# Rotary embedding on one core: the first batch row loaded by one GpSimd cast transfer instead of two transfers on two queues

## The chip, the cores and the metric

One core of one Trainium2 chip. The metric is device time in microseconds (us), the median of several runs of the whole kernel, inputs and outputs in HBM.

## The reference

The kernel rotates pairs of neighbouring elements. `x` is 8 x 2048 x 16 x 64 in fp32 (batch, sequence, heads, head size), `cos` and `sin` are 2048 x 32:

```python
x_pairs = x.reshape(batch, seq_len, num_heads, head_dim // 2, 2)
x1 = x_pairs[..., 0]
x2 = x_pairs[..., 1]
out1 = x1 * cos - x2 * sin      # cos, sin: one value per position and pair
out2 = x1 * sin + x2 * cos
out = np.stack([out1, out2], axis=-1).reshape(batch, seq_len, num_heads, head_dim)
```

`x` and `out` are 67.1 MB each.

## The kernel before

The sequence is split over 128 partitions, 16 positions on each, so a batch row of `x` is a tile of 128 x 16384 elements: 8.39 MB in fp32 in HBM, half of that in bf16 in the core. The kernel works in bf16. A transfer issued by GpSimd (the helpers `load` and `store`) changes fp32 to bf16 on the way in and back on the way out.

`xt` holds five such rows (slots); `HOME` says which slot each of the eight batch rows uses, so rows 5, 6 and 7 go into the slots of rows 0, 1 and 2 once those are stored. `c_tab` and `s_tab` hold the cosines and signed sines in bf16, each value twice. `rotate(b)` does three VectorE instructions on a row: L89 writes `qt` = x * `s_tab`, L92 writes x = x * `c_tab` in place, L97 adds `qt` with the neighbours swapped to x. `qt` is one buffer of the pool `stage`.

The order is written out by hand (`manual_schedule`); each engine does its instructions in the order of the code.

- Head: the first row comes in two parts. Positions 0 to 3 of each partition (`HEAD` = 4, 2.10 MB of fp32) are loaded by SyncE without a cast (L101) into the buffer `head` (named `st` in the profile), which shares its room with `qt`, and ScalarE casts them into `xt` (L108). Positions 4 to 15 come by a GpSimd cast transfer (L102). Behind that on GpSimd's queue stand cos (L103), sin (L104), rows 1 and 2 in one transfer (`load(1, 2)`, L70), and rows 3 and 4 (`load(3, 2)`).
- VectorE builds the tables (L110 to L112), then does rotate(0) in two pieces (positions 0 to 3, then 4 to 15), then rows 1 to 7 in one piece each.
- Stores by GpSimd (L74): row 0 is issued behind the first instruction of rotate(2), through two one-element ScalarE copies (L120, L121) that hold it back; rows 1 and 2 after rotate(2); rows 3 and 4 after rotate(4); rows 5 and 6 after rotate(6). Row 5 is loaded once row 0 is stored, rows 6 and 7 once rows 1 and 2 are.
- End: ScalarE casts row 7 to fp32 in four parts (L138) into the room of slots 3 and 4, and SyncE stores it (L139).

Of the kernel before, what the change touches and what calls it, by code (L numbers as in the profile page):

```python
# [2 lines left out]

# [4 lines left out]


@with_exitstack  # L10
def kernel(
    ctx: ExitStack,
    tc: tile.TileContext,
    x: bass.AP,
    cos: bass.AP,
    sin: bass.AP,
    out: bass.AP,
):
    nc = tc.nc
    fp32 = mybir.dt.float32  # L20
    bf16 = mybir.dt.bfloat16
    mult = mybir.AluOpType.mult
    add = mybir.AluOpType.add

    B, S, H, D = x.shape
    P = 128
    K = S // P
    KP = 16
    D2 = D // 2
    HD = H * D  # L30
    NX = 5
    HEAD = 4
    PART = 4
    STAGE = 3


    HOME = [0, 1, 2, 3, 4, 0, 1, 2]

    x_t = x.rearrange("b (p k) h d -> b p k (h d)", p=P, k=K)
    out_t = out.rearrange("b (p k) h d -> b p k (h d)", p=P, k=K)  # L40
    x_r = x.rearrange("b (p k) h d -> p b (k h d)", p=P, k=K)
    out_r = out.rearrange("b (p k) h d -> p b (k h d)", p=P, k=K)
    cos_t = cos.rearrange("(p k) c -> p (k c)", p=P, k=K)
    sin_t = sin.rearrange("(p k) c -> p (k c)", p=P, k=K)

    consts = ctx.enter_context(tc.tile_pool(name="consts", bufs=1))
    stage = ctx.enter_context(tc.tile_pool(name="stage", bufs=1))

    xt = consts.tile([P, NX, K * HD], bf16)
    cos_sb = consts.tile([P, K * D2], fp32)  # L50
    sin_sb = consts.tile([P, K * D2], fp32)
    c_tab = consts.tile([P, K, D], bf16)
    s_tab = consts.tile([P, K, D], bf16)

    wide = (
        xt[:, STAGE : STAGE + 2]
        .rearrange("p a c -> p (a c)")
        .bitcast(fp32)
        .rearrange("p (k c) -> p k c", c=HD)
    )  # L60

    gate = consts.tile([1, 1], bf16)
    mark = consts.tile([1, 1], bf16)

    def home(b, k0=0, k1=K):
        return xt[:, HOME[b], k0 * HD : k1 * HD].rearrange("p (k c) -> p k c", c=HD)

    def load(b, n):
        h = HOME[b]
        nc.gpsimd.dma_start(out=xt[:, h : h + n], in_=x_r[:, b : b + n])  # L70

    def store(b, n):
        h = HOME[b]
        nc.gpsimd.dma_start(out=out_r[:, b : b + n], in_=xt[:, h : h + n])  # L74

    def rotate(b, k0=0, k1=K, between=None):
        nk = k1 - k0
        xp = home(b, k0, k1)
        qt = stage.tile([P, KP, HD], bf16, name="qt", tag="work")

        def rows(a):
            return a.rearrange("p k (h e) -> p k h e", h=H, e=D)

        def tab(a):
            return dataclasses.replace(
                a, offset=a.offset + k0 * D, ap=[a.ap[0], [D, nk], [0, H], [1, D]]
            )

        nc.vector.tensor_tensor(out=rows(qt[:, :nk]), in0=rows(xp), in1=tab(s_tab), op=mult)  # L89
        if between is not None:  # L90
            between(qt)
        nc.vector.tensor_tensor(out=rows(xp), in0=rows(xp), in1=tab(c_tab), op=mult)  # L92
        q_swap = dataclasses.replace(
            qt, offset=qt.offset + 1, ap=[qt.ap[0], [2, nk * HD // 2], [-1, 2]]
        )
        x3 = xp.rearrange("p k (a j) -> p (k a) j", j=2)
        nc.vector.tensor_tensor(out=x3, in0=x3, in1=q_swap, op=add)  # L97

    with tc.manual_schedule():
        head = stage.tile([P, HEAD, HD], fp32, name="st", tag="work")  # L100
        nc.sync.dma_start(out=head[:, :HEAD], in_=x_t[0, :, :HEAD])  # L101
        nc.gpsimd.dma_start(out=home(0, HEAD), in_=x_t[0, :, HEAD:])  # L102
        nc.gpsimd.dma_start(out=cos_sb, in_=cos_t)  # L103
        nc.gpsimd.dma_start(out=sin_sb, in_=sin_t)  # L104
        load(1, 2)
        load(3, 2)

        nc.scalar.copy(out=home(0, 0, HEAD), in_=head[:, :HEAD])  # L108
        s2 = s_tab.rearrange("p k (i j) -> p (k i) j", j=2)
        nc.vector.tensor_copy(out=s2[:, :, 0], in_=sin_sb)  # L110
        nc.vector.tensor_scalar_mul(s2[:, :, 1], sin_sb, -1.0)  # L111
        nc.vector.tensor_copy(  # L112
            out=c_tab.rearrange("p k (i j) -> p (k i) j", j=2),
            in_=cos_sb.to_broadcast([P, K * D2, 2]),
        )
        rotate(0, 0, HEAD)
        rotate(0, HEAD, K)

        def first_store(qt):
            nc.scalar.copy(out=gate, in_=qt[:1, KP - 1, HD - 1 :])  # L120
            nc.scalar.copy(out=xt[:1, HOME[0], :1], in_=xt[:1, HOME[0], :1])  # L121
            store(0, 1)

        rotate(1)
        rotate(2, between=first_store)
        nc.gpsimd.tensor_copy(out=mark, in_=xt[:1, 4, K * HD - 1 :])  # L126
        store(1, 2)
        load(5, 1)
        load(6, 2)
        rotate(3)  # L130
        rotate(4)
        store(3, 2)
        for b in range(5, B):
            rotate(b)
            if b == 6:
                store(5, 2)
        for k in range(0, K, PART):
            nc.scalar.copy(out=wide[:, k : k + PART], in_=home(B - 1, k, k + PART))  # L138
        nc.sync.dma_start(out=out_t[B - 1], in_=wide)  # L139


# [1 line left out]
_INS = ['x', 'cos', 'sin']  # L143
_OUTS = [((8, 2048, 16, 64), 'float32')]


# [23 lines left out]
```

## Time and profile before

| | |
|---|---|
| median of 3 runs | 316.28 us (316.09 to 316.48) |
| span of the profiled execution, first to last instruction | 314.3 us |
| the median stands above that span by | 1.98 us |
| busy in the span | VectorE 210.3 us, ScalarE 19.3 us, GpSimd 12.4 us |
| transfers, counted as written | GpSimd's queue (q0) 91.75 MB, SyncE's (q1) 10.49 MB |

The profile gives no separate time for its own execution; its span is set against the median of the runs. In the profile DVE is VectorE, ACT is ScalarE, POOL is GpSimd and SP is SyncE; a letter q behind an engine means its queue. The DMA share is the mean over the core's 16 DMA engines, in the rows by slices in tenths, in the rows by stretches as a fraction. A transfer's packets are counted where they start, so a very short stretch can show a share above 1. A wait is put down to what ended it.

### The profile page before, as it was taken

How to read it: one execution, taken by the hardware profiler on the slowest of the kernel's cores; microseconds unless marked ns; L12 is line 12 of the kernel's file. 1: busy time of each engine (PE TensorE's matmuls, PEld its weight loads, DVE VectorE, ACT ScalarE, POOL GpSimd, SP SyncE). 2: the span in 40 equal slices, each digit the busy share in tenths (PEclk: the TensorE clock that was granted, in tenths of full speed). 3: DMA queues.
4: the chain of work that ended last, by engine and by line, in shares of the span. 5: the costliest groups of instructions: out<-in, count | busy, mean ns of one | idle time of the engine just before them, and what ended most of it. 6: DMA issues, size and time to landing. Idle time of an engine off the chain costs nothing.

```text
span 314.3 us, 114 instructions
## 1 busy us (share of the span) xinstructions
DVE 210.3 (67%) x30; ACT 19.3 (6%) x8; POOL 12.4 (4%) x16
## 2 busy tenths in 40 slices
DVE  0009995099999999999992299903999999200000
ACT  1030000000000000000000000000000000790000
POOL 4000000000002400000000000000000000000000
DMA  7999999999999999999999999999999999999996
GB/s 253 264 284 200 200 200 267 200 200 204 263 200 267 409 525 400 400 425 509 400 200 225 242 200 200 234 234 334 400 509 425 400 400 525 409 400 400 525 409 267
DMA packets 2512, 102.24 MB, mean 325 GB/s; under 512 B 208, under 2 KB 208, under 8 KB 336
## 3 DMA queue, kind: packets, MB, share of 16 engines
q0 software_dynamic: 2224, 91.75, 92.1%
q1 hardware_dynamic: 288, 10.49, 8.0%
HBM read 67.63 MB, written 67.11 MB: 429 GB/s over the span
## 4 chain that ended last, share of the span: by engine, by line
DVE 67%; another core or an unknown queue 11%; ACT 3%; ACTq 1%; issue 0%; DVEq 0%
DVE xt L92 22%; DVE xt L97 22%; DVE qt L89 22%; ACT xt L138 3%; ACTq L165 1%; DVE c_tab L112 0%; DVEq L89 0%; DVEq L92 0%
## 5 line engine op out<-in xcount | busy, mean ns | idle before, releaser
L89 DVE TENSOR_TENSOR qt<-xt,s_tab 128x16384 bf16<-128x16384 bf16 (+2 forms) x9 | 69.7, 7743 | 34.5 <-DMA xt<-in_x_dram 34.3
L92 DVE TENSOR_TENSOR xt<-xt,c_tab 128x16384 bf16<-128x16384 bf16 (+2 forms) x9 | 69.7, 7743 | 0.4
L97 DVE TENSOR_TENSOR xt<-xt,qt 128x16384 bf16<-128x16384 bf16 (+2 forms) x9 | 69.7, 7743 | 0.3
L138 ACT CAST xt<-xt 128x4096 f32<-128x4096 bf16 x4 | 14.1, 3601 | 171.7 <-DVE xt L97 171.7
L110 DVE CAST s_tab<-sin_sb 128x512 bf16<-128x512 f32 x1 | 0.5, 454 | 23.8 <-DMA sin_sb<-in_sin_dram 23.8
L74 POOL DMA_DIRECT2D out_dram<-xt x4 | 2.7, 670 | 184.9 <-ACT xt L121 93.4
L126 POOL COPY mark<-xt 1x1 bf16<-1x1 bf16 x1 | 5.0, 5019 | 2.6 <-DMA xt<-in_x_dram 2.6
L120 ACT COPY gate<-qt 1x1 bf16<-1x1 bf16 x1 | 0.2, 192 | 78.6 <-DVE qt L89 78.6
L70 POOL DMA_DIRECT2D xt<-in_x_dram x4 | 2.7, 696 | 43.1 <-DMA out_dram<-xt 43.1
L108 ACT CAST xt<-st 128x4096 bf16<-128x4096 f32 x1 | 3.6, 3605 | 13.1 <-DMA st<-in_x_dram 13.1
L108 ACT ACT_TABLE_LOAD x1 | 1.3, 1283 | 0.7 <-PEq L154 0.7
L102 POOL DMA_DIRECT2D xt<-in_x_dram x1 | 0.7, 680 | 0.8 <-PEq L165 0.8
L112 DVE CAST c_tab<-cos_sb 128x1024 bf16<-128x1024 f32 x1 | 0.7, 685 | 0.0
L103 POOL DMA_DIRECT2D cos_sb<-in_cos_dram x1 | 0.6, 569 | 0.0
L104 POOL DMA_DIRECT2D sin_sb<-in_sin_dram x1 | 0.6, 562 | 0.0
L111 DVE TENSOR_SCALAR s_tab<-sin_sb 128x512 bf16<-128x512 f32 x1 | 0.4, 444 | 0.0
L121 ACT COPY xt<-xt 1x1 bf16<-1x1 bf16 x1 | 0.2, 188 | 0.0
L154 POOL MEMSET const-float32-0.0<- 128x1 f32 x1 | 0.1, 99 | 0.2 <-issue 0.2
L154 POOL MEMSET const-bfloat16-1.0<- 128x1 bf16 x1 | 0.1, 102 | 0.0
L154 POOL MEMSET const-float32-1.0<- 128x1 f32 x1 | 0.1, 99 | 0.0
L154 POOL MEMSET const-uint8-127<- 128x1 uint8 x1 | 0.1, 99 | 0.0
## 6 DMA issues: line engine op xcount, KB each, us to landing
xt<-in_x_dram POOLq DMA_DIRECT2D x3, 8192.0 KB, 59.3
xt<-in_x_dram POOLq DMA_DIRECT2D x1, 4096.0 KB, 57.6
xt<-in_x_dram POOLq DMA_DIRECT2D x1, 3072.0 KB, 21.1
st<-in_x_dram SPq DMA_DIRECT2D x1, 2048.0 KB, 14.4
cos_sb<-in_cos_dram POOLq DMA_DIRECT2D x1, 256.0 KB, 21.2
sin_sb<-in_sin_dram POOLq DMA_DIRECT2D x1, 256.0 KB, 21.3
out_dram<-xt POOLq DMA_DIRECT2D x4, 49.9
out_dram<-xt SPq DMA_DIRECT2D x1, 30.0
```

The costliest lines, as they stand in the source:

```text
L70: nc.gpsimd.dma_start(out=xt[:, h : h + n], in_=x_r[:, b : b + n])
L74: nc.gpsimd.dma_start(out=out_r[:, b : b + n], in_=xt[:, h : h + n])
L89: nc.vector.tensor_tensor(out=rows(qt[:, :nk]), in0=rows(xp), in1=tab(s_tab), op=mult)
L92: nc.vector.tensor_tensor(out=rows(xp), in0=rows(xp), in1=tab(c_tab), op=mult)
L97: nc.vector.tensor_tensor(out=x3, in0=x3, in1=q_swap, op=add)
L102: nc.gpsimd.dma_start(out=home(0, HEAD), in_=x_t[0, :, HEAD:])
L103: nc.gpsimd.dma_start(out=cos_sb, in_=cos_t)
L108: nc.scalar.copy(out=home(0, 0, HEAD), in_=head[:, :HEAD])
L112: nc.vector.tensor_copy(out=c_tab.rearrange("p k (i j) -> p (k i) j", j=2), in_=cos_sb.to_broadcast([P, K * D2, 2]),)
L126: nc.gpsimd.tensor_copy(out=mark, in_=xt[:1, 4, K * HD - 1 :])
L138: nc.scalar.copy(out=wide[:, k : k + PART], in_=home(B - 1, k, k + PART))
L165: with _tile.TileContext(nc) as tc:
```

## The change

The first row is loaded by one GpSimd cast transfer of the whole row, `load(0, 1)`. SyncE's uncast part, its buffer and ScalarE's cast are taken out, and rotate(0) works on the whole row in one piece.

```diff
-    HEAD = 4
...
-    x_t = x.rearrange("b (p k) h d -> b p k (h d)", p=P, k=K)
...
     with tc.manual_schedule():
-        head = stage.tile([P, HEAD, HD], fp32, name="st", tag="work")
-        nc.sync.dma_start(out=head[:, :HEAD], in_=x_t[0, :, :HEAD])
-        nc.gpsimd.dma_start(out=home(0, HEAD), in_=x_t[0, :, HEAD:])
+        load(0, 1)
         nc.gpsimd.dma_start(out=cos_sb, in_=cos_t)
         nc.gpsimd.dma_start(out=sin_sb, in_=sin_t)
         load(1, 2)
         load(3, 2)
 
-        nc.scalar.copy(out=home(0, 0, HEAD), in_=head[:, :HEAD])
         s2 = s_tab.rearrange("p k (i j) -> p (k i) j", j=2)
...
-        rotate(0, 0, HEAD)
-        rotate(0, HEAD, K)
+        rotate(0)
```

The order of all other instructions on each engine is the same as before.

## The prediction

> **What bounds the kernel now.** I read the page's DMA rows first, then its chain, then the trace in stretches. The page:
>
> ```profile
> DVE 210.3 (67%) x30; ACT 19.3 (6%) x8; POOL 12.4 (4%) x16
> DMA  7999999999999999999999999999999999999996
> HBM read 67.63 MB, written 67.11 MB: 429 GB/s over the span
> DVE 67%; another core or an unknown queue 11%; ACT 3%; ACTq 1%; issue 0%; DVEq 0%
> ```
>
> The chain (last line) names VectorE, but VectorE works two thirds of the span, while the 16 DMA engines are full in every slice but the first and the last. So I ask of the trace whether the DMA engines ever rest. The busy time in stretches, cut where one transfer follows another (columns: length, VectorE, ScalarE, GpSimd, clock, DMA share, GB/s):
>
> ```profile
> 23.10:61.60 38.50, 27.82 (x9) 0.00 (x0) 0.00 (x0) 1.00 1.00 216
> 61.60:100.34 38.74, 37.78 (x5) 0.29 (x2) 0.55 (x1) 1.00 1.01 217
> 100.34:119.70 19.36, 19.24 (x3) 0.00 (x0) 5.72 (x2) 1.00 1.02 437
> 119.70:158.30 38.60, 38.39 (x5) 0.00 (x0) 0.57 (x1) 1.00 1.02 434
> 254.80:312.80 58.00, 14.44 (x2) 14.12 (x4) 0.00 (x0) 1.00 1.01 434
> ```
>
> GB/s counts the bytes as written. A cast load reads twice what it writes, so 216 to 217 is 433 read; stores write 434 to 437. Each fp32 byte costs the same whether loaded with a cast, stored, or (last stretch, where the SyncE store runs with a GpSimd one) moved by either queue. In order: load(1,2), load(3,2), store(0,1), store(1,2), and at the end store(5,2) with the last store; each stretch is as long as its bytes at 434 GB/s. The transfers stand in one line from 23.1 us to the end with no rest. VectorE waits for the line: 10.66 us before batch 1, 11.17 before batch 5, 12.42 before batch 6. The kernel's time is therefore when the DMA engines start, plus all the bytes at 434 GB/s, plus a short end. No byte between HBM and the core is added or removed by this change, so what counts is how the first 23 us are filled.
>
> **The first stretch.** The timeline at the start, then three answers in narrow stretches:
>
> ```profile
> 0.74 0.37 SPq L101 DMA_DIRECT2D st<-in_x_dram  x1
> 1.25 0.68 POOL L102 DMA_DIRECT2D xt<-in_x_dram  x1 [0.81 <-PEq L165]
> ...
> 1.50:1.70 0.20, 0.00 (x0) 0.20 (x1) 0.20 (x1) 1.00 0.00 0
> 1.70:1.80 0.10, 0.00 (x0) 0.10 (x1) 0.10 (x1) 1.00 3.85 819
> ...
> DMA packets 80, 1.31 MB, mean 345 GB/s; under 512 B 0, under 2 KB 0, under 8 KB 0
> q1 hardware_dynamic: 80, 1.31, 96.8%
> ```
>
> SyncE's transfer is issued at 0.74 and its first data moves at 1.74: 1.00 us. The last two lines are the DMA rows of 1.5 to 5.3 us: only SyncE's queue (q1) has moved anything, 80 packets of 16 KB, five on each engine. GpSimd's transfer, issued at 1.25, first shows at 5.42 (nothing starts in 5.3 to 5.4; in 5.4 to 5.8 q0 has 15 packets). Until then SyncE's part is what keeps the engines at work.
>
> **The change, part by part.**
>
> *SyncE's transfer goes, its 2.10 MB move into the first cast transfer.* Same fp32 bytes, same rate, so no change in work: two kinds of packet in turn against one kind, both near 434. I book nothing for the difference, with 0.2 us either way. What is lost is the work done before the cast transfer starts: 1.31 MB / 434 GB/s = 3.02 us. In the changed kernel the engines start empty. If the first cast data moves at S, and its cold start costs c, then the state of 5.42 is reached at S + c + 3.02, and everything behind it is late by
>
> d = S + c - 2.40.
>
> *c.* SyncE's 1.31 MB took 5.42 - 1.74 = 3.68 us instead of 3.02: 0.66 us of cold start. A cast transfer on cold engines may pay the same or nothing: 0 to 0.66, and I take 0.6, because its row is the only cold start in the trace.
>
> *S.* The trace has no GpSimd transfer that meets idle engines. Upper end: 5.42, as now. Lower end: GpSimd as quick as SyncE, 1.25 + 1.00 = 2.25. Between them lie two rows. First, store(0,1) is issued by GpSimd at 97.91 and its first packets, one on each engine, start in 100.3 to 100.7 (about 100.36), right behind the last of load(3,2): it was ready within 2.45 us of its issue. That puts S at 1.25 + 2.45 = 3.70 at most, if the first GpSimd transfer is no slower than a later one. Second, the engines seem to take up packets ahead. The last store is issued by SyncE at 283.46, so by the 1.00 us above it was ready at about 284.5. Yet the rows say:
>
> ```profile
> q0 software_dynamic: 32, 2.10, 73.1%
> ...
> q1 hardware_dynamic: 16, 1.05, 98.0%
> ```
>
> From 284.2 to 290.9 each engine still started two GpSimd packets (32), and SyncE's began only in 290.9 to 293.4. A newcomer waits two more packets behind the running one. Put that on the head: five SyncE packets ran first, so the cast transfer was ready while the third ran, which is 3.5 to 4.2 us (the third and fourth rounds of 16 KB packets start at about 3.56 and 4.18). The two rows meet at S = 3.6.
>
> The Trainium skill, page "DMA: Bandwidth & Descriptors", section "Queues, rings and completion order", says that each DMA engine goes round robin over the queues that have work, packet by packet. Read strictly, with no packets taken ahead, it would put S at 5.42, or one SyncE packet earlier at 4.8; the row of 32 packets at the end speaks against the strict reading.
>
> So d = 3.6 + 0.6 - 2.40 = 1.8 us. From both sides: 2.25 + 0 - 2.40 = -0.15, and 5.42 + 0.66 - 2.40 = 3.7.
>
> *ScalarE's cast (3.6 us, L108) goes.* It ran from 15.16 to 18.76, off the path: VectorE starts at 23.77, when sin lands. Worth 0; so is the staging buffer, which nothing had to wait for. The table load at the start stays, hidden in 25 us of waiting.
>
> *rotate(0) in one piece.* Three instructions of 128x16384 at 8.69 us (26.1) for 3 x 2.29 and 3 x 6.56 (26.6): 0.5 us less on VectorE. It still starts when sin lands, behind the same bytes, and ends 10.66 us before load(1,2) lands; all of it goes into that wait. It needs the whole first row where before it needed a quarter, but the tables are queued behind that row and VectorE's order has them first, so nothing new is waited for. If the cover were gone it would be a gain of 0.5, not a loss.
>
> *GpSimd's queue.* Still five loads in the same order, the first larger by a third; its issue instruction may grow from 0.68 to the 0.72 of a pair of rows, and that is inside S. Behind load(1,2) everything hangs on its landing: VectorE, the issue of store(0,1), the issue of the later loads. All shift by d together, and the reserves (store(1,2) is issued at 115.04, needed at 119.7; store(5,2) at 243.40, needed at 254.8; the last store at 283.46, needed when store(5,2) alone would end, about 293) stay as they are. The narrowest is store(0,1): 97.91 against 100.34, just its own readiness.
>
> Sum: span 314.3 + 1.8 = 316.1. The median of the runs, 316.28, stands 1.98 above the span; with that kept, 318.1 us. A measurement of this kernel can tell about 0.2% from no change, 0.63 us.
>
> **The rivals.**
>
> *The cast transfer is ready late (slower by more).* It first shows at 5.42 because only then is it ready. For it: nothing of it moved earlier, and the first GpSimd transfer of a program may be slower than one at 98 us. Against it: store(0,1) within 2.45 us, and the two packets taken ahead. S = 4.8 to 5.42 gives d = 3.0 to 3.7 with c, 319.5. Chance 0.18.
>
> *The queue hardly matters (no change).* Only the later issue is lost, 1.25 - 0.74 = 0.51 us, and both start cold alike: S = 2.25, c = 0.66, d = 0.5, 316.8. For it: the issues stand that close. Against it: GpSimd's issue instruction itself lasts until 1.93. The same page, section "Issuing engines are not separate DMA queues", says that spreading transfers over engines saves only the time to initiate them, which would be this rival; the rows of 1.5 to 5.3 us show 3.68 us in which only one queue moved data. Chance 0.16, taken for all d within 0.63.
>
> *Faster.* The cast transfer starts as early as SyncE's did, at 1.74, and warm: d = 1.74 - 2.40 = -0.66, 315.6. It decides at the start: the first cast data must move before 1.77 us with no cold cost. Against it: the instruction that issues it is only over at 1.93. Chance 0.03.
>
> *The narrow place breaks.* If store(0,1) came late to the line, the engines would idle from 100.3 on, on top of the 1.8: with 2 us late, 320.1. Against it: it and load(3,2) hang on the same load(1,2). Chance 0.03.
>
> **How the numbers follow.** The forecast (S from 3.0 to 4.2, c from 0 to 0.66, d = 0.6 to 2.5) has the remaining 0.60 and gives 318.1. The range goes from 316.6, part of the no-change case, to 319.6, most of the late case. Slower: 0.60 + 0.18 + 0.03 = 0.81; same 0.16; faster 0.03.
>
> **What would show it.** In the changed profile: DMA share 0 until the first cast packets at about 3.6 us; the queues at 92.8 MB (q0) and 8.39 MB (q1), since 1.05 MB of bf16 comes to q0 and 2.10 leave q1; VectorE's wait for sin 25.6 instead of 23.8; its wait before batch 1 at 11.2 (10.66 + 0.5); the waits before batches 5 and 6 unchanged at 11.2 and 12.4; ScalarE's first cast gone; span 316.1. First cast data before 2.4 us, or an unchanged landing of sin, makes the prediction wrong at S; a shift at sin that differs from the shift of the end makes the one-line argument wrong.

## The result and the profile after

The changed kernel takes 317.23 us (median of 7 runs, 317.11 to 317.95), the kernel before 316.48 beside it (7 runs, 316.09 to 317.0). The ratio is 1.0033, 95% interval 1.0023 to 1.0042: slower by 0.75 us. The span of the profiled execution went from 314.3 to 315.3 us.

Lines of the page of the changed kernel:

```profile
DVE 209.9 (67%) x27; ACT 15.7 (5%) x7; POOL 12.4 (4%) x16
DMA  7979999999999999999999999999999999999996
q0 software_dynamic: 2224, 92.80, 93.6%
q1 hardware_dynamic: 144, 8.39, 6.2%
HBM read 67.63 MB, written 67.11 MB: 427 GB/s over the span
```

The same bytes went through HBM, 1.05 MB of bf16 came to q0 and 2.10 MB left q1, as foreseen. The new thing is the 133 GB/s in the first slice, where it was 253. The 7 in the third slice is no rest: packets are counted where they start, and the second slice stands at 1.18, the third at 0.79, together full (in e7 below, the same kernel, they read 9 and 8). The head in narrow stretches (columns: length, VectorE, ScalarE, GpSimd, clock, DMA share, GB/s as written):

```profile
2.50:2.60 0.10, 0.00 (x0) 0.00 (x0) 0.10 (x1) 1.00 0.00 0
2.60:3.10 0.50, 0.00 (x0) 0.00 (x0) 0.50 (x2) 1.00 6.45 1049
3.10:5.70 2.60, 0.00 (x0) 0.00 (x0) 1.38 (x2) 1.00 0.00 0
5.70:6.30 0.60, 0.00 (x0) 0.00 (x0) 0.00 (x0) 1.00 4.06 874
```

The first 16 cast packets, one on each engine, start from 2.63 us on. Their successors start from 5.71 on. From 3.10 to 5.70 nothing starts, since the packets are under way (they are counted where they start). A packet of this size later follows its predecessor after 2.43 us, so the first one costs 3.08 - 2.43 = 0.65 more, counted between first starts. Packet by packet, the 16 first ones took 3.06 to 3.49 us, 3.22 in the mean. The timeline over the head:

```profile
1.25 0.68 POOL L68 DMA_DIRECT2D xt<-in_x_dram  x1 [0.81 <-PEq L159]
...
24.88 0.45 DVE L105 CAST s_tab<-sin_sb 128x512 bf16<-128x512 f32 x1 [24.88 <-DMA sin_sb<-in_sin_dram]
...
63.49 8.69 DVE L87 TENSOR_TENSOR qt<-xt,s_tab 128x16384 bf16<-128x16384 bf16 x1 [11.20 <-DMA xt<-in_x_dram]
```

Sin lands 1.1 us later than before (24.88 against 23.77), row 1 too (63.49 against 62.42), and the last store is issued 1.1 later (284.56 against 283.46); the span is 1.0 longer. Behind the head the stretches are as long as they were:

```profile
120.55:159.15 38.60, 38.39 (x5) 0.00 (x0) 0.58 (x1) 1.00 1.01 432
255.75:313.70 57.95, 14.60 (x2) 14.12 (x4) 0.00 (x0) 1.00 1.00 431
```

So the loss arises before the second cast packets, which start at 5.71 to 6.29 us, and is carried to the end.

### The profile page after: what moved, and what is told of

The parts are those of the page before. It is cut to its first block, busy times and chain, and to the rows that moved or that the text cites. A ratio compares the mean times of both kernels' runs of the same rounds, so it can differ in the third digit from the quotient of the medians.

```text
span 315.3 us, 107 instructions
## 1 busy us (share of the span) xinstructions
DVE 209.9 (67%) x27; ACT 15.7 (5%) x7; POOL 12.4 (4%) x16
## 4 chain that ended last, share of the span: by engine, by line
DVE 67%; another core or an unknown queue 11%; DMA 7%; ACT 3%; ACTq 1%; issue 1%; POOL 0%; DVEq 0%; PEldq 0%
DVE xt L90 22%; DVE xt L95 22%; DVE qt L87 22%; DMA sin_sb<-in_sin_dram 7%; ACT xt L132 3%; ACTq L159 1%; POOL xt L68 0%; DVE c_tab L107 0%; POOL cos_sb L99 0%; DVE s_tab L106 0%; DVEq L87 0%; DVE s_tab L105 0%; DVEq L90 0%; PEldq L159 0%
## 5 line engine op out<-in xcount | busy, mean ns | idle before, releaser
L87 DVE TENSOR_TENSOR qt<-xt,s_tab 128x16384 bf16<-128x16384 bf16 x8 | 69.5, 8692 | 35.0 <-DMA xt<-in_x_dram 34.8
L90 DVE TENSOR_TENSOR xt<-xt,c_tab 128x16384 bf16<-128x16384 bf16 x8 | 69.5, 8692 | 0.3
L95 DVE TENSOR_TENSOR xt<-xt,qt 128x16384 bf16<-128x16384 bf16 x8 | 69.5, 8692 | 0.3
```

## The experiments

The theory ("empty start"): the DMA engines work without rest from their first data to the end, so what the change costs is the time in which they stand empty or cold until the first cast data. The rival ("whole first row"): what costs is that the row must land whole, and VectorE's later or undivided start on it. Ratios are against runs of the kernel before on the same chip, made beside those of the experiment. The profile does not name the DMA engine of a packet; "on each engine" below is worked out from the counts and from packets that follow one another.

### e6: the kernel before with rotate(0) in one piece

```diff
-        rotate(0, 0, HEAD)
-        rotate(0, HEAD, K)
+        rotate(0)
```

> The kernel before with rotate(0) in one piece, SyncE's part and ScalarE's cast kept. Theory 'empty start': no change, ratio 0.999 to 1.001, with 0.5 us more of VectorE's wait before batch 1. Rival 'whole first row': this part of the change alone gives its loss, 1.003.

Measured 316.19 us, ratio 1.0002 (0.9993 to 1.0011). VectorE's timeline of this kernel:

```profile
62.51 8.69 DVE L89 TENSOR_TENSOR qt<-xt,s_tab 128x16384 bf16<-128x16384 bf16 x1 [11.19 <-DMA xt<-in_x_dram]
```

The 0.5 us saved on VectorE lies in its wait, 11.19 for 10.66. This part of the change is worth nothing.

### e2 and e5: GpSimd's first load issued 1.38 us later

The same edit, ahead of GpSimd's first load, once in the changed kernel (e2) and once in the kernel before (e5):

```diff
+        nc.gpsimd.memset(c_tab, 0.0)
+        nc.gpsimd.memset(c_tab, 0.0)
```

> The changed kernel, with two GpSimd memsets of c_tab (overwritten later, so the result is untouched) ahead of the first load, which delay its issue by their time D, read from the profile; I expect about 2 us. Theory 'empty start': the DMA engines are the line that sets the end, so the end moves by D, one for one, 317.2 + D. Rival 'hidden': VectorE's wait of 11.2 us before batch 1 takes the delay up, 317.2.

> The kernel before (SyncE's part of 2.10 MB kept), with the same two GpSimd memsets of c_tab ahead of GpSimd's first load, so that its first load is issued 1.38 us later, at 2.63. Theory 'empty start': SyncE's part alone keeps the engines at work from 1.74 to about 1.74 + 0.65 + 4.8 = 7.2, the cast transfer is ready at 2.63 + 1.38 = 4.0, so nothing is lost: the time of the kernel before, 316.2 (ratio 0.999 to 1.001), where the same delay cost the changed kernel 1.3 to 1.7. Rival 'GpSimd's queue is the line': + 1.4, 317.6 (ratio 1.0044). The first cast packets: if the engines take up 64 KB ahead of a newcomer (as 4 x 16 KB in the kernel before, 2 x 32 KB with HEAD = 8), then the third SyncE packet runs at 4.0 and the cast follows the seventh, at about 6.7; if the first five always go first, 5.4.

e2: 318.49 us, ratio 1.0077 (1.0065 to 1.0089), against 1.0033 and, in e7, 1.0043 for the changed kernel itself: 0.0034 to 0.0044 more, which is 1.1 to 1.4 us of 316.2. The timeline has the load issued at 2.63 instead of 1.25, 1.38 later where about 2 was expected, and the stretches of this kernel show its first data at 4.0 instead of 2.63:

```profile
3.95:4.00 0.05, 0.00 (x0) 0.00 (x0) 0.05 (x1) 1.00 0.00 0
4.00:4.50 0.50, 0.00 (x0) 0.00 (x0) 0.50 (x2) 1.00 6.22 1049
4.50:6.90 2.40, 0.00 (x0) 0.00 (x0) 1.36 (x2) 1.00 0.00 0
```

The time moves about one for one with the first cast data, though VectorE still waits 11.23 us before batch 1 and could have taken up the delay.

e5: 316.16 us, ratio 1.0003 (0.9995 to 1.0012). With SyncE's 2.10 MB under way the same delay costs nothing. Its DMA rows, first of 1.5 to 6.5 us, then of 6.5 to 6.9:

```profile
q1 hardware_dynamic: 112, 1.84, 96.3%
...
q0 software_dynamic: 11, 0.27, 314.9%
q1 hardware_dynamic: 2, 0.03, 19.1%
```

112 SyncE packets are seven on each engine, and the two behind them an eighth on two engines; the first cast packet starts at 6.55 (6.7 was expected). Together the pair shows what SyncE's part did: it covered the time until the cast transfer was ready.

### e8: the changed kernel with SyncE's part as mere cover

```diff
+    x_t = x.rearrange("b (p k) h d -> b p k (h d)", p=P, k=K)
...
+        head = stage.tile([P, 4, HD], fp32, name="st", tag="work")
+        nc.sync.dma_start(out=head, in_=x_t[0, :, :4])
         load(0, 1)
```

> The changed kernel, with SyncE's part of 2.10 MB issued ahead as in the kernel before, into a buffer that nothing reads: the whole row still comes by the GpSimd cast transfer, so 2.10 MB more are moved in all, 2.10 / 434 GB/s = 4.83 us (eight packets of 0.61 us on each engine: 4.9). Theory 'empty start': with the engines covered from 1.74 until the cast transfer is ready nothing else is lost, 316.16 + 4.83 = 321.0 (ratio 1.0148 to 1.0160). Rival 'the one cast transfer of the whole row costs in itself' (it must land whole, VectorE starts on it later): the changed kernel's 317.3 + 4.83 = 322.1 (ratio 1.018 to 1.019).

Measured 321.26 us, ratio 1.0160 (1.0146 to 1.0174). Taking off the added bytes' 4.83 leaves 316.43, 0.24 above the kernel before beside it (316.19), where the changed kernel lies 0.75 to 1.22 above. The rival's 1.018 is outside the interval. In the trace the 16 engines' last completions come 4.92 later in the mean than in the kernel before, and eight packets were expected to take 4.9. With the engines covered, one cast transfer for the whole row costs little or nothing in itself.

### e3 and e4: other sizes of SyncE's part in the kernel before

```diff
-    HEAD = 4
+    HEAD = 1
```

This is e3; in e4 HEAD is 8.

> The kernel before with HEAD = 1: SyncE's uncast part is 0.52 MB in 4 KB packets, eight on each engine, instead of 2.10 MB. Theory 'empty start' with the cast transfer ready at 2.65 as in the changed kernel: SyncE's part lasts from 1.74 to 1.74 + 0.65 + 1.2 = 3.6, the cast transfer takes over without a rest, 316.5 (ratio 0.999 to 1.001). Rival 'ready late beside SyncE': the cast transfer was at 5.42 in the kernel before because SyncE's issue delays its descriptors; then the engines rest from 3.6 to 5.4 and the time is 316.5 + 1.8 = 318.3. If instead five SyncE packets always go first, the first cast packet is at about 1.74 + 0.65 + 5 x 0.15 = 3.1.

> The kernel before with HEAD = 8: SyncE's uncast part is 4.19 MB in 32 KB packets. Theory 'empty start': same first data at 1.74, same bytes, no rest: 316.5 (ratio 0.999 to 1.001). The place of the first cast packet tells what 'five SyncE packets first' was: five packets again puts it at 1.74 + 0.65 + 5 x 1.21 = 8.4, a fixed number of bytes (80 KB per engine) at about 6.0, a fixed time at 5.4. Rival 'whole first row' (the later the first cast positions are needed, the better): 316.5 as well, with VectorE's start at sin unchanged.

e4: 316.31 us, ratio 1.0008 (0.9999 to 1.0016), as expected. Its DMA rows of 1.5 to 6.0 us, in which no cast packet started:

```profile
DMA packets 48, 1.57 MB, mean 350 GB/s; under 512 B 0, under 2 KB 0, under 8 KB 0
q1 hardware_dynamic: 48, 1.57, 93.7%
```

Three packets of 32 KB on each engine, and the first cast packet at 6.00. Five packets (8.4) are out, and it was 96 KB on each engine, not 80, that went first.

e3: 316.59 us, ratio 1.0014 (1.0005 to 1.0023), against an expected 0.999 to 1.001, so 0.4 us slower. The rival of a transfer made late by SyncE (318.3) is out: each engine took up its cast packet when its eight small SyncE packets were gone, from 3.61 us on. But these packets lasted until 4.05 and not 3.6. That 4 KB packets pay more for a cold start is my reading of it; no run separates it.

### e1 and e9: the changed kernel with cos and sin by SyncE

```diff
-        nc.gpsimd.dma_start(out=cos_sb, in_=cos_t)
-        nc.gpsimd.dma_start(out=sin_sb, in_=sin_t)
+        nc.sync.dma_start(out=cos_sb, in_=cos_t)
+        nc.sync.dma_start(out=sin_sb, in_=sin_t)
```

> The changed kernel, with cos and sin loaded by SyncE instead of GpSimd (no other change). Theory 'empty start': what was lost is the time in which the DMA engines have nothing to do before the first cast data (2.64 us, then a cold start of 0.65), so 0.52 MB from SyncE that begins at 1.74 us fills it: 0.52 / 434 GB/s = 1.2 us plus 0.65 cold reaches 3.6, past 2.65, no rest, and the end comes where it did in the kernel before, 316.5 us (ratio 0.999 to 1.001), or 0.75 under the changed kernel. Rival 'whole first row': VectorE's later start on a row that must land whole is what costs; row 0 still lands whole and last, so the time stays at 317.2 (ratio 1.003).

> The kernel of e1 once more (cos and sin by SyncE, 0.52 MB). There SyncE's packets were used up at 3.6, when the cast transfer was only just ready; 11 of the 16 DMA engines ended before the ends of the kernel before, five later, the last by 0.9 us. If the cover is merely too short, the same again: first cast packets above 2.44 us on several engines, the median of the engines' ends at that of the kernel before, the last one 0.5 or more later, time 316.6 to 317.2. If the e1 profile was one odd execution, the ends lie as close as in the kernel before and the time is 316.2.

Measured 317.0 us, ratio 1.0032 (1.002 to 1.0043), then 317.6, ratio 1.0043 (1.0031 to 1.0056). My theory had said 316.5; the number came out where the rival had it. The rival's reason does not hold (e6, e8), so I looked at the head of e9, stretches and then the DMA rows of 3.7 to 5.9 us:

```profile
3.40:3.70 0.30, 0.00 (x0) 0.00 (x0) 0.00 (x0) 1.00 6.75 1461
3.70:4.10 0.40, 0.10 (x1) 0.00 (x0) 0.00 (x0) 1.00 0.00 0
4.10:4.60 0.50, 0.50 (x2) 0.00 (x0) 0.00 (x0) 1.00 1.55 262
4.60:5.80 1.20, 0.76 (x2) 0.00 (x0) 0.00 (x0) 1.00 0.00 0
...
DMA packets 4, 0.13 MB, mean 60 GB/s; under 512 B 0, under 2 KB 0, under 8 KB 0
q0 software_dynamic: 4, 0.13, 35.3%
```

SyncE's packets are used up at 3.64. Twelve engines start their cast packets in 3.4 to 3.7. Four do so only at 4.15 to 4.56, 0.5 to 0.9 us after SyncE's last packet, and their first packets take 2.9 to 3.2 us instead of 2.43. The end of this kernel, DMA rows of 312.6 to 313.9 and of 314 to 315 (one completion packet for each engine):

```profile
q1 hardware_dynamic: 12, 0.00, 0.5%
...
q1 hardware_dynamic: 4, 0.00, 0.2%
```

Twelve engines end at 313.1 to 313.5, four at 314.1 to 314.6: four latecomers of the head, four at the end. That they are the same four is inferred from the count: where the first stores start, twelve engines and four stand as far apart (100.69 to 102.18 us) as at the end. In e1, twelve end by 312.9 (the kernel before: 312.8 to 313.1), four at 313.4 to 314.0; there no first cast packet starts later than 3.85, but four of them take 2.98 to 3.39 us.

So this cover by cos and sin was not enough, and it fails on a few engines, which suffices. The expectation of e9 was missed too: 317.6 is above its 317.2, and the median of the engines' ends is 0.4 later than in the kernel before, not at it. A cast transfer that is ready at 2.63 should have taken over at 3.64 on every engine; why four got their first cast packet late stays open.

### e7: the changed kernel again

> The changed kernel once more, on the chip and beside the runs of the other kernels here: ratio 1.002 to 1.004 as before. In its trace I look at when each of the 16 DMA engines ends its last packet: if the end is set by the slowest engine, the spread of these ends explains why the span moved by 1.0 us and the first engine's line by 0.84.

Measured 317.38 us, ratio 1.0043 (1.003 to 1.0055), a little over the expected 1.004. The first of its 16 engines ends at 313.47, the last at 314.30, where in the kernel before they lie between 312.78 and 313.11, and in the first trace of the changed kernel between 313.62 and 314.16. In all three the distance between first and last is in place where the first stores start, by 102 us, and the same to 0.02 us at the end. The mean of the 16 ends is 0.90 later than in the kernel before in the first trace of the changed kernel and 0.89 in this one.

No run points to a version that beats the kernel before: e4, e5 and e6 equal it, and in none did data move earlier than SyncE's in the kernel before, but for 0.01 us.

## Why the prediction was right, and which term was mis-sized

*What bounds.* Right. The DMA engines are one line without rest: a delay at the head comes out at the end although VectorE waits 11 us (e2), and vanishes where the engines have other work (e5). The shift at sin (1.11) and that of the span (1.0) agree to 0.1 us, as the one-line argument asks.

*Work.* Nothing booked for the bytes, and nothing seen: the stretches behind the head kept their lengths.

*c.* 0.6 taken, 0.65 measured between first starts.

*S, the term that was off.* 3.6 taken, 2.63 measured: 1.38 us from GpSimd's issue to its data, against SyncE's 1.00. With it the same formula gives d = 2.63 + 0.65 - 2.40 = 0.88. Measured are 0.75 and 1.22 between medians, and 1.0 between the spans. The forecast was 1.8, about twice the size, and its range from 316.6 held the time. Part of that is luck: 2.63 lies outside the 3.0 to 4.2 that the forecast allowed for S, and d still fell within its 0.6 to 2.5 because c came out at the top of its bounds.

Two steps led S astray. The bound from store(0,1), 2.45 us after its issue, was only a bound, and I took the value at its end. And the step "a newcomer waits two more packets behind the running one" counted packets where the rows fit bytes. In the kernel before, 16 KB packets: if the cast transfer is ready at 2.63 as in the changed kernel, in the first packet, then four more go first. In e4, 32 KB packets: also ready in the first, two more go first. In e5, ready at 4.0 in the third of 16 KB, and it is taken after the seventh: four more. At the end of the kernel, two store packets, of 32 KB each as read. Each time 64 KB as read are ahead on most engines (a few let one packet more go first). Read so, the 80 SyncE packets of the prediction put S inside the first packet, before about 2.9.

That the count of packets is not fixed is shown: with the cast transfer issued at the same 1.25, five of 16 KB go first, or three of 32 KB. That the limit is one of bytes read is inferred from these four places and leans on the readiness taken over from the changed kernel; beside SyncE's packets the runs show only that it was ready by 3.36 (the first cast packet of e1). A fixed time of 2.2 to 2.5 us up to the next packet boundary would fit the three heads as well, but not the end, where SyncE's packets began 6.5 us after their estimated readiness at 284.5.

The Trainium skill, page "DMA: Bandwidth & Descriptors", section "Queues, rings and completion order", has the engines change queues after each packet. The runs agree once both queues are at work (in the kernel before, SyncE's packets of 0.62 us and cast packets of 1.83 us take turns from 5.42 on), but not for a newcomer: in e5 the cast transfer was due at 4.0, the first data of e2 with the same issue time, and first moved at 6.55. The Trainium skill, same page, section "Specifications", gives about 1 us to the first byte by GpSimd's path and about 0.6 by SyncE's. Here they are 1.38 and 1.00 from the start of the issuing instruction to the first data: the difference agrees, both are 0.4 longer.

*The covers.* Right: rotate(0) in one piece (wait 11.20, forecast 11.2), ScalarE's cast at nothing (no run takes it out alone, but e8, which has none, is late by little more than its added bytes), the reserves unchanged, store(0,1) still in time.

*What was missing.* The step "the state of 5.42 is reached later, and everything behind it is late by d" treats 16 engines as one. The last engine sets the end: the formula's 0.88 is what the mean of the 16 ends moved by (0.90 and 0.89 in the two traces of the changed kernel), while the first engine's end moved by 0.84 and 0.69 and the last one's by 1.0 and 1.2.

*The rivals.* "Ready late" fell with the first cast data at 2.63. "The queue hardly matters", d = 0.5, came closer in time (316.8 against 317.23) than the forecast: of the loss, 0.51 us is the later issue, 0.38 the longer way from issue to data, and the cold start falls on both kernels nearly alike (0.66 and 0.65). "Faster" would have needed data by 1.77.

## What to carry to other kernels

Where the DMA engines are the line from start to end, look at the first microseconds: a small transfer on the queue that gets its data first can be worth the time until the larger one is ready, here 0.75 to 1.22 us of 316, if it keeps all 16 engines at work until then (2.10 MB did, 0.52 MB did not quite). Removing an engine's cast that is off the path brought nothing, and joining two transfers lost what the first one covered. When a bound from the trace is one-sided, take a value inside it, not at its end.

## What the runs showed of the hardware

A newly issued transfer did not start at the next packet boundary of a busy DMA engine: about 64 KB as read went first. The same GpSimd load, issued at 1.25, first moved at 2.63 on idle engines (the changed kernel), at 3.36 behind 32 KB of small SyncE packets on each engine (e1) and at 5.39 behind 16 KB packets (e8), so the 5.42 of the kernel before said little of when its cast transfer was ready. And a lag that one of the 16 engines picks up at the head was not made up: in e9 first and last engine were 1.49 us apart where the first stores start and 1.49 at the last completions.
